# A two-layer hybrid block in fp32: another order of making the scaled blocks of the gated stage

## The chip, the cores and the metric

The kernel runs on 1 core of one Trainium2 chip. The metric is the device time of one execution in microseconds (us): before the change 2495.34 us, the median of 3 runs (2489.96 to 2497.64).

## The reference

One sequence of T = 1024 tokens with D = 1024 features goes through two layers. Layer 0 mixes tokens with two kinds of attention, layer 1 with a chunkwise mLSTM; both are followed by the same gated stage of hidden width 2816, whose beginning the change touches. Everything is fp32.

```python
for layer in range(DEPTH):                      # DEPTH = 2
    hn = rmsnorm(h, norm_mix[layer])
    h = h + mixer[layer](hn)                    # nsa_swa_mixer, then mlstm_mixer
    h = h + swiglu(rmsnorm(h, norm_ffn[layer]),
                   ffn_w_gate[layer], ffn_w_up[layer], ffn_w_down[layer])
return rmsnorm(h, final_norm)

def rmsnorm(x, g):
    return x * rsqrt(mean(x * x, axis=-1) + RMS_EPS) * g
def swiglu(x, wg, wu, wd):
    return (silu(x @ wg) * (x @ wu)) @ wd
```

## The kernel before

**Layout.** Activations lie transposed: 8 chunks of 128 features (on the partitions) by two token halves of 512, `h[hf][c]`. In the trace these tiles are named `r`.

**Products.** An fp32 product is made of three TensorE matmuls, high part by high part, high by low, low by high. The high part is a cast on ScalarE (`hi_copy`, L119), the low part a subtraction on VectorE that reads the cast (`lo_sub`, L124). So every operand and every weight costs one instruction on each of these engines before TensorE can use it. Operands split in this way are tiles `y`, weights split in this way `wh` (four chunks of weights, four such tiles in turn) and `whl` (eight chunks). Raw weights, `ws`, are loaded by SyncE's queue (L137).

**The gated stage** takes the hidden features 128 at a time, `m` = 0 to 21, in this program order:

- `ffn_head`: m = 0 and 1 on token half 0. The operand here was already split, without the factor 1/rms; the factor comes in behind the product (L284). Products go to `pg` and `pu` (L179 to L181).
- `rb(hf)` makes that factor for a half: a matmul with a matrix of ones sums the squares (`nrm`, L267), VectorE L269, ScalarE Ln (L271) and Exp (L272), each with a table load, then VectorE L274, L275, L277 into `consts`.
- `operands`, first part: for half 1, each chunk is multiplied in place by its norm weight and 1/rms (L953), all eight chunks, in the order 0, 4, 1, 5 and so on; then the eight results are split (L119, L124).
- `gated_rest`: m = 0 and 1 on half 1, 4 products of 24 matmuls, tiles `pr` (L983 to L985), each out of two halves of weights that are split when they are called for.
- `operands`, the rest: half 0 is scaled and one of its two blocks split, and the sums and differences of blocks (tiles `m`, L961 to L972) that the next step needs are made and split.
- `gated2`, m = 2 to 20 in steps of two: `wino` makes a 2 x 2 block product out of 7 instead of 8 block products (Winograd's form), for gate and for up. The seven operand blocks come in the order B11, T2, T1, B21, T3, T4, B22; B.. are blocks of the scaled input, T.. sums of them. A product is 12 matmuls into tiles `wb`, on lines L983 to L985 too. Their weights are sums of quarters of the raw weights (tiles `s`, L997) or the quarters, split one by one ahead of each product.

**What sets the order.** A scheduler turns the program order into one in-order queue for each engine, and adds the semaphore waits. An instruction that waits holds everything behind it on its engine. In layer 0 the second head (m = 1) stands in between the last products of the mixer; in layer 1 the mixer is done before `ffn_head` begins.

Of the kernel before, what the change touches and what calls it, by code (L numbers as in the profile page):

```python
# [25 lines left out]
NC = D // P  # L26
# [10 lines left out]
class Net:  # L37
# [753 lines left out]
    def mixer_ab(self):  # L791
# [3 lines left out]
        with tc.tile_pool(name="at", bufs=1) as self.at:  # L795
# [42 lines left out]
            next(last)  # L838
            head = self.ffn_head(0)
            next(head)  # L840
            for step in last:
                if step:
                    self.square(self.h[1][step[0]], 1)
            next(head)

    def ab_out(self, chunks, hfs):

# [94 lines left out]
        self.hi_copy(hi, x, "act")  # L942
        self.lo_sub(lo, x, hi)

    def operands(self, layer):

        nc = self.nc
        self.B = {}
        b = {}
        for hf in (1, 0):  # L950
            for c in (0, 4, 1, 5, 2, 6, 3, 7):
                x = b[c // 4, hf, c % 4] = self.h[hf][c]
                nc.vector.scalar_tensor_tensor(x, x, self.v("nf", layer * NC + c), self.rb(hf), op0=OP.mult, op1=OP.mult)  # L953
            for k in range(2):
                if hf or k == 0:
                    for j in range(4):
                        self.operand(f"B{k + 1}{hf + 1}", j, b[k, hf, j])
            yield
        t1, t2 = self.four(), self.four()
        for j in range(4):  # L960
            nc.vector.tensor_sub(t1[j], b[0, 1, j], b[0, 0, j])  # L961
            nc.vector.tensor_sub(t2[j], b[1, 1, j], t1[j])
            self.operand("T2", j, t2[j])
        for j in range(4):
            self.operand("T1", j, t1[j])
        for j in range(4):
            self.operand("B21", j, b[1, 0, j])
# [6 lines left out]
        yield  # L974
# [12 lines left out]
    def wino(self, st, out):  # L987
# [14 lines left out]
        def prod(ps, w, n, first=True):  # L1002
            self.half_products(ps, w, self.B[n], first)

        c11, u2, u3, c22 = self.four()
        a = bank()
        prod(a, a11, "B11")
        nc.scalar.copy(u3, a)
        s1, s2 = pair()
        combine(s1, a21, a22, OP.add)  # L1010
        combine(s2, s1, a11, OP.subtract)
        b = bank()
        prod(b, s2, "T2")
        nc.vector.tensor_add(u2, u3, b)
        c = bank()
        prod(c, s1, "T1")
        prod(a, a12, "B21", False)
        out(0, 0, a, c11)
        s3, s4 = pair()
        combine(s3, a11, a21, OP.subtract)  # L1020
# [11 lines left out]
        out(0, 1, u2, u2)  # L1032
        return (c11, u2), (u3, c22)

    def gated2(self, wg, wu, m):
# [12 lines left out]

        g = self.wino(sts[0], gate)
        self.wino(sts[1], up)  # L1050

    def gated_rest(self, wg, wu):
# [3 lines left out]
        for i in range(2):  # L1056
# [7 lines left out]
            nc.vector.tensor_mul(u, g, p[1])  # L1064
            self.hid_out(u, i, 1)

    def ffn(self, layer, last, head=False):
        nc, a = self.nc, self.a
        wg, wu, wd = (a[f"ffn_w_{n}"][layer] for n in ("gate", "up", "down"))
        if last:  # L1070
            self.park_tokens()
        else:
            for hf in range(2):
                for c in range(NC):
                    nc.sync.dma_start(self.spill[c][:, hf * H5:(hf + 1) * H5], self.h[hf][c])
# [12 lines left out]
        if last:  # L1088
# [490 lines left out]
```

## Time and profile before

| | before |
|---|---|
| median of 3 runs | 2495.34 us (2489.96 to 2497.64) |
| the profiled execution, its own time | 2500.09 us |
| its span in the trace | 2498.4 us |
| mean granted TensorE clock, share of full | 0.978 |
| busy: TensorE, VectorE, ScalarE, GpSimd | 95%, 65%, 36%, 20% of the span |

The profiled execution is one more run, 4.75 us above the median. Its own time is 1.7 us more than the span that its instructions cover. Engines are named as in the profile: PE is TensorE (PEld its weight loads), DVE VectorE, ACT ScalarE, POOL GpSimd, SP SyncE. A row of a timeline gives the start, the duration from first start to last end, and in brackets the idle time before it with what ended it. Matmul records last longer than the distance from one to the next, so pace is read from the distance of starts.

### The profile page before, as it was taken

How to read it: one execution, taken by the hardware profiler on the slowest of the kernel's cores; microseconds unless marked ns; L12 is line 12 of the kernel's file. 1: busy time of each engine (PE TensorE's matmuls, PEld its weight loads, DVE VectorE, ACT ScalarE, POOL GpSimd, SP SyncE). 2: the span in 40 equal slices, each digit the busy share in tenths (PEclk: the TensorE clock that was granted, in tenths of full speed). 3: DMA queues.
4: the chain of work that ended last, by engine and by line, in shares of the span. 5: the costliest groups of instructions: out<-in, count | busy, mean ns of one | idle time of the engine just before them, and what ended most of it. 6: DMA issues, size and time to landing. Idle time of an engine off the chain costs nothing.

```text
span 2498.4 us, 29577 instructions
## 1 busy us (share of the span) xinstructions
PE 2377.8 (95%) x10729; PEld 1899.5 (76%) x10729; DVE 1630.7 (65%) x2817; ACT 894.9 (36%) x1851; POOL 503.7 (20%) x606
## 2 busy tenths in 40 slices
PE   7999998998869999999999999999979999999998
PEld 5778776776658888887777788888857888887886
DVE  6545766687786666668876554554386666567867
ACT  5234655566252222222222344332253232222222
POOL 3134654444300000003322111111100000002322
PEclk9999989999989999999999999999989999999999
DMA  5623742211423433449333211122233434348443
GB/s 188 196 66 110 210 109 70 77 53 30 140 74 121 166 123 130 150 153 325 121 135 100 62 43 38 38 70 86 65 121 102 148 106 159 127 170 290 137 146 114
DMA packets 246757, 304.20 MB, mean 122 GB/s; under 512 B 19076, under 2 KB 157524, under 8 KB 246612
## 3 DMA queue, kind: packets, MB, share of 16 engines
q1 hardware_dynamic: 246612, 302.31, 37.5%
q8 instruction: 85, 1.39, 0.2%
q14 instruction: 60, 0.49, 0.1%
HBM read 218.33 MB, written 83.90 MB: 121 GB/s over the span
## 4 chain that ended last, share of the span: by engine, by line
PE 78%; DVE 8%; POOL 5%; issue 4%; ACT 3%; DMA 2%; SPq 0%; DVEq 0%; POOLq 0%; ACTq 0%
PE dn L1153 14%; PE wb L983 10%; PE wb L985 10%; PE wb L984 10%; PE acc L181 4%; PE acc L180 4%; PE acc L179 4%; PE acc L190 2%; PE acc L188 2%; PE acc L189 2%; PE T L701 2%; PE S L610 2%; POOL e L684 2%; PE po L695 1%; PE po L696 1%
## 5 line engine op out<-in xcount | busy, mean ns | idle before, releaser
L985 PE MATMUL wb<-y,wh 128*128 128x512 f32 x1120 | 442.3, 395 | 19.9 <-DVE wh L124 19.9
L983 PE MATMUL wb<-y,wh 128*128 128x512 f32 x1120 | 442.9, 395 | 1.3 <-DVE m L1023 1.2
L984 PE MATMUL wb<-y,wh 128*128 128x512 f32 x1120 | 443.0, 396 | 0.0
L117 POOL TENSOR_SCALAR wo<-ws 128x1024 fp32r<-128x1024 f32 x84 | 124.1, 1489 | 1114.1 <-DMA ws<-in_ffn_w_down 507.1
L985 PEld LDWEIGHTS wb<-y,wh 128*128 128x128 f32 x1120 | 211.7, 189 | 69.6 <-DVE wh L124 20.8
L983 PEld LDWEIGHTS wb<-y,wh 128*128 128x128 f32 x1120 | 211.4, 189 | 53.2 <-issue 4.3
L984 PEld LDWEIGHTS wb<-y,wh 128*128 128x128 f32 x1120 | 211.4, 189 | 48.1
L1153 PE MATMUL dn<-xo,wo 128*128 128x512 f32 x924 | 220.0, 401 | 6.2 <-DVE wo L124 6.1
L1153 PE MATMUL dn<-wo,xo 128*128 128x512 f32 x924 | 215.7, 395 | 2.2 <-ACT xo L119 2.1
L1153 PEld LDWEIGHTS dn<-xo,wo 128*128 128x128 f32 x924 | 176.9, 192 | 49.3 <-DVE wo L124 7.4
L1153 PEld LDWEIGHTS dn<-wo,xo 128*128 128x128 f32 x924 | 173.8, 188 | 44.0 <-issue 2.5
L179 PE MATMUL acc<-x,whl 128*128 128x512 f32 x416 | 170.4, 410 | 0.0
L180 PE MATMUL acc<-x,whl 128*128 128x512 f32 x416 | 166.3, 400 | 0.0
L181 PE MATMUL acc<-x,whl 128*128 128x512 f32 x416 | 165.4, 398 | 0.0
L188 PE MATMUL acc<-x,whl 128*128 128x512 f32 x384 | 158.2, 412 | 4.0 <-DMA x<-os 2.6
L189 PE MATMUL acc<-x,whl 128*128 128x512 f32 x384 | 155.3, 404 | 3.3 <-DMA x<-os 2.0
L684 POOL TENSOR_SCALAR e<-e,st 128x256 f32<-128x256 f32 (+7 forms) x192 | 121.6, 652 | 173.2 <-ACT oc L716 40.0
L124 DVE TENSOR_TENSOR wh<-ws,wh 128x512 fp32r<-128x512 f32 x136 | 93.0, 687 | 94.1 <-ACT wh L119 94.1
L190 PE MATMUL acc<-x,whl 128*128 128x512 f32 x384 | 153.6, 400 | 0.7 <-DVE whl L124 0.7
L119 ACT CAST xo<-hb 128x1024 fp32r<-128x1024 f32 x84 | 79.3, 975 | 205.5 <-PE dn L1153 134.9
L706 DVE TENSOR_TENSOR eh<-T,eh 128x512 fp32r<-128x512 f32 (+1 forms) x178 | 120.4, 687 | 48.5 <-ACT eh L705 47.1
L610 PE MATMUL S<-kv,qa 128*128 128x256 f32 (+3 forms) x528 | 124.4, 331 | 10.2 <-ACT ec L627 2.9
(335 smaller groups left out, 4414.8 us busy)
## 6 DMA issues: line engine op xcount, KB each, us to landing
ws<-in_ffn_w_down SPq DMA_DIRECT2D x34, 1024.0 KB
ws<-in_ffn_w_gate SPq DMA_DIRECT2D x22, 1024.0 KB
ws<-in_ffn_w_up SPq DMA_DIRECT2D x22, 1024.0 KB
sd<-m SPq DMA_DIRECT2D x22, 1024.0 KB
hs<-m SPq DMA_DIRECT2D x80, 256.0 KB
qa<-qs SPq DMA_DIRECT2D x128, 128.0 KB
hb<-hs SPq DMA_DIRECT2D x16, 1024.0 KB
ws<-sd SPq DMA_DIRECT2D x16, 1024.0 KB
```

Of the source, the lines that this page charges most:

```text
L179: nc.tensor.matmul(ps, w[:, 0, k], xh, start=(start and k == 0), stop=False)
L180: nc.tensor.matmul(ps, w[:, 0, k], xl, start=False, stop=False)
L181: nc.tensor.matmul(ps, w[:, 1, k], xh, start=False, stop=(stop and k == n - 1))
L188: self.nc.tensor.matmul(ps, w[:, 0, i], xh, start=i == 0, stop=False)
L189: self.nc.tensor.matmul(ps, w[:, 0, i], xl, start=False, stop=False)
L190: self.nc.tensor.matmul(ps, w[:, 1, i], xh, start=False, stop=i == len(xs) - 1)
L610: nc.tensor.matmul(p[:, at + c:at + c + k.shape[1]], qq[:, r * P:(r + 1) * P], k, start=i == 0, stop=i == 1, skip_group_check=True)
L684: self.last_scale = nc.gpsimd.tensor_scalar(es[r][:, :w], es[r][:, :w], f[:, r:r + 1], 0.0, op0=OP.mult, op1=OP.add)
L983: nc.tensor.matmul(ps, t[:, 0, k], xh, start=first and k == 0, stop=False, skip_group_check=True)
L984: nc.tensor.matmul(ps, t[:, 0, k], xl, start=False, stop=False, skip_group_check=True)
L985: nc.tensor.matmul(ps, t[:, 1, k], xh, start=False, stop=last and k == 3, skip_group_check=True)
L1153: nc.tensor.matmul(ps[i], l, r, start=first and k == 0 and q == 0, stop=end and k == 10 and q == 2, skip_group_check=True)
```

## The change

Three things are done in another order. (1) `rb(1)` is called right behind the first head, and the parking of `h` in memory behind it, ahead of the scaling. (2) `operands` becomes `scaled(layer, hf)`, which scales one chunk and splits it at once, chunks in the order 0 to 7, with half 1 ahead of the second head and half 0 behind it, both ahead of `gated_rest`; and `sums`, which makes the sums of blocks. (3) `sums` is called inside the first `gated2`, behind the splitting of the weights of its first four products (`half_parts` for a11, s2, s1, a12), no longer ahead of it. The number of instructions on each engine stays the same.

```diff
@@ mixer of layer 0
             head = self.ffn_head(0)
             next(head)
+            self.B = {}
             for step in last:
                 if step:
                     self.square(self.h[1][step[0]], 1)
+            self.rb(1)
+            for hf in range(2):
+                self.park(hf)
+            self.scaled(0, 1)
             next(head)
+            self.scaled(0, 0)
@@
-    def operands(self, layer):
-        nc = self.nc
-        self.B = {}
-        b = {}
-        for hf in (1, 0):
-            for c in (0, 4, 1, 5, 2, 6, 3, 7):
-                x = b[c // 4, hf, c % 4] = self.h[hf][c]
-                nc.vector.scalar_tensor_tensor(x, x, self.v("nf", layer * NC + c), self.rb(hf), op0=OP.mult, op1=OP.mult)
-            for k in range(2):
+    def scaled(self, layer, hf):
+        for k in range(2):
+            for j in range(4):
+                x = self.h[hf][4 * k + j]
+                self.nc.vector.scalar_tensor_tensor(x, x, self.v("nf", layer * NC + 4 * k + j), self.rb(hf),
+                                                    op0=OP.mult, op1=OP.mult)
                 if hf or k == 0:
-                    for j in range(4):
-                        self.operand(f"B{k + 1}{hf + 1}", j, b[k, hf, j])
-            yield
+                    self.operand(f"B{k + 1}{hf + 1}", j, x)
+
+    def sums(self):
+        nc = self.nc
+        b = {(k, n, j): self.h[n][4 * k + j] for k in range(2) for n in range(2) for j in range(4)}
         t1, t2 = self.four(), self.four()
...
-    def half_products(self, ps, w, x, first=True, last=True):
+    def half_parts(self, w):
         t = self.small_w()
         self.hi_copy(t[:, 0], w, "act")
         self.lo_sub(t[:, 1], w, t[:, 0])
+        return t
+
+    def half_products(self, ps, w, x, first=True, last=True, t=None):
+        if t is None:
+            t = self.half_parts(w)
@@ wino
+        t = [None] * 4
+        if between:
+            t[0] = self.half_parts(a11)
         s1, s2 = pair()
         combine(s1, a21, a22, OP.add)
         combine(s2, s1, a11, OP.subtract)
+        if between:
+            t[1:] = [self.half_parts(w) for w in (s2, s1, a12)]
+            between()
@@ ffn
         if not head:
-            for _ in self.ffn_head(layer):
-                pass
-        steps = self.operands(layer)
-        next(steps)
+            if last:
+                self.park_tokens()
+            else:
+                for hf in range(2):
+                    self.park(hf)
+            self.B = {}
+            steps = self.ffn_head(layer)
+            next(steps)
+            self.scaled(layer, 1)
+            next(steps)
+            self.scaled(layer, 0)
         self.gated_rest(wg[:, :2 * P], wu[:, :2 * P])
-        for _ in steps:
-            pass
         for m in range(2, 22, 2):
-            self.gated2(wg[:, m * P:(m + 2) * P], wu[:, m * P:(m + 2) * P], m)
+            self.gated2(wg[:, m * P:(m + 2) * P], wu[:, m * P:(m + 2) * P], m, self.sums if m == 2 else None)
```

What the queues hold, at three places. The first is VectorE in layer 0, from the second head to the scaled chunks of half 1. Before, `u` and `pu` belong to the head, `r` and `rm` to the chunks and to `rb`:

```order
L284 TENSOR_TENSOR u<-pu,consts 128x512
L922 TENSOR_TENSOR u<-g,u 128x512
L269 TENSOR_SCALAR rm<-nrm 128x512
L274 TENSOR_TENSOR rm<-rm,r_6919 128x512
L275 SCALAR_TENSOR_TENSOR rm<-rm,r_6919 128x512
L277 SCALAR_TENSOR_TENSOR consts<-rm,r_6919 128x512
L953 SCALAR_TENSOR_TENSOR r<-r,consts 128x512 x8
L124 TENSOR_TENSOR y<-r,y 128x512 x8
L124 TENSOR_TENSOR wh<-ws,wh 128x512
```

In the change the same engine at the same place, first the rows that make 1/rms:

```order
L269 TENSOR_SCALAR rm<-nrm 128x512
L124 TENSOR_TENSOR whl<-ws,whl 128x1024
L274 TENSOR_TENSOR rm<-rm,r_6835 128x512
L124 TENSOR_TENSOR wh<-ws,wh 128x512
L275 SCALAR_TENSOR_TENSOR rm<-rm,r_6835 128x512
L284 TENSOR_TENSOR g<-pg,consts 128x512
L277 SCALAR_TENSOR_TENSOR consts<-rm,r_6835 128x512
```

and then, behind one more `wh`, the rows of the chunks:

```order
L956 SCALAR_TENSOR_TENSOR r<-r,consts 128x512 x3
L124 TENSOR_TENSOR y<-r,y 128x512 x3
L956 SCALAR_TENSOR_TENSOR r<-r,consts 128x512 x3
L124 TENSOR_TENSOR y<-r,y 128x512 x3
L956 SCALAR_TENSOR_TENSOR r<-r,consts 128x512 x2
L284 TENSOR_TENSOR u<-pu,consts 128x512
L124 TENSOR_TENSOR y<-r,y 128x512 x2
L928 TENSOR_TENSOR u<-g,u 128x512
L124 TENSOR_TENSOR y<-r,y 128x512 x4
L124 TENSOR_TENSOR wh<-ws,wh 128x512 x4
```

L953 has become L956. The factor stands ahead of the head's two rows `u`, with one split of gated-rest weights `wh` inside it and one behind it; scaling and splitting take turns, and four chunks of half 0 (`y` x4) stand ahead of the next four `wh`.

The second place is VectorE in layer 1. Before, two pairs of `wh` (the weights of `gated_rest`) stand ahead of the factor of half 1:

```order
L953 SCALAR_TENSOR_TENSOR r<-r,consts 128x512 x3
L124 TENSOR_TENSOR wh<-ws,wh 128x512 x2
L953 SCALAR_TENSOR_TENSOR r<-r,consts 128x512 x3
L284 TENSOR_TENSOR u<-pu,consts 128x512
L269 TENSOR_SCALAR rm<-nrm 128x512
L922 TENSOR_TENSOR u<-g,u 128x512
L274 TENSOR_TENSOR rm<-rm,r_14685 128x512
L275 SCALAR_TENSOR_TENSOR rm<-rm,r_14685 128x512
L277 SCALAR_TENSOR_TENSOR consts<-rm,r_14685 128x512
L953 SCALAR_TENSOR_TENSOR r<-r,consts 128x512 x8
L124 TENSOR_TENSOR y<-r,y 128x512 x8
L124 TENSOR_TENSOR wh<-ws,wh 128x512
```

In the change, from the end of the factor on:

```order
L277 SCALAR_TENSOR_TENSOR consts<-rm,r_14618 128x512
L956 SCALAR_TENSOR_TENSOR r<-r,consts 128x512 x4
L124 TENSOR_TENSOR y<-r,y 128x512 x3
L956 SCALAR_TENSOR_TENSOR r<-r,consts 128x512 x3
L124 TENSOR_TENSOR y<-r,y 128x512 x3
L956 SCALAR_TENSOR_TENSOR r<-r,consts 128x512 x2
L284 TENSOR_TENSOR u<-pu,consts 128x512
L124 TENSOR_TENSOR y<-r,y 128x512 x2
L928 TENSOR_TENSOR u<-g,u 128x512
L124 TENSOR_TENSOR y<-r,y 128x512 x4
L956 SCALAR_TENSOR_TENSOR r<-r,consts 128x512 x2
L124 TENSOR_TENSOR wh<-ws,wh 128x512 x4
```

The first `wh` of `gated_rest` now stands behind all of these, and the factor and its `nrm` matmul ahead of the second head's products.

The third place is ScalarE in layer 0 around the first `gated2`. `m` are the sums of blocks and the results of products, `s` the sums of weights. Before, all casts of sums stand ahead of the first weights:

```order
L119 CAST y<-m 128x512 x4
L119 CAST y<-r 128x512 x4
L119 CAST y<-m 128x512 x8
L119 CAST wh<-s 128x512 x2
L119 CAST wh<-ws 128x512
L1008 COPY m<-wb 128x512
L119 CAST wh<-s 128x512
```

In the change, from the last of the first four weights (`wh<-ws`) to the weights of T3 (the first `wh<-s` here):

```order
L119 CAST wh<-ws 128x512
L119 CAST y<-r 128x512 x2
L1028 COPY m<-wb 128x512
L119 CAST y<-m 128x512 x6
L1058 ACTIVATE m<-wb 128x512
L119 CAST y<-m 128x512 x2
L119 CAST wh<-s 128x512
```

Four weights moved ahead of the sums; the weights of the fifth product, T3, stand behind the casts of T3 and T4 and behind the silu L1058 of the result that comes out of the fourth product.

## Rows read from the trace of the kernel before

**Rows 1.** The page: busy time of each engine, and the chain's shares.

```profile
PE 2377.8 (95%) x10729; PEld 1899.5 (76%) x10729; DVE 1630.7 (65%) x2817; ACT 894.9 (36%) x1851; POOL 503.7 (20%) x606
...
PE 78%; DVE 8%; POOL 5%; issue 4%; ACT 3%; DMA 2%; SPq 0%; DVEq 0%; POOLq 0%; ACTq 0%
```

**Rows 2.** Waits of 640 to 780 us, layer 0: us in total, times, longest.

```profile
PE wb L985 <- DVE wh L124: 10.0, 1, 10.0
```

**Rows 3.** Windows: PE, PEld, DVE, ACT, POOL busy; granted clock, DMA share, GB/s.

```profile
696.00:712.00 16.00, 4.45 (x10) 3.12 (x11) 13.22 (x21) 10.07 (x17) 0.00 (x0) 0.57 0.27 82
...
732.00:746.00 14.00, 4.05 (x11) 2.93 (x10) 13.90 (x25) 5.83 (x11) 0.00 (x0) 0.63 0.05 19
...
1831.00:1849.00 18.00, 6.90 (x17) 4.91 (x17) 15.86 (x26) 10.88 (x17) 0.00 (x0) 0.62 0.04 15
...
1868.00:1883.00 15.00, 5.05 (x13) 3.85 (x13) 15.00 (x26) 6.63 (x12) 0.00 (x0) 0.66 0.05 17
```

**Rows 4.** Timeline of PE in layer 0.

```profile
694.90 1.02 PE L267 MATMUL nrm<-consts 128*128 128x512 f32 x2
704.18 1.22 PE L983 MATMUL pr<-y,wh 128*128 128x512 f32 x2 [8.25 <-ACT y L119]
708.77 0.80 PE L984 MATMUL pr<-y,wh 128*128 128x512 f32 x1 [3.37 <-DVE y L124]
709.36 0.63 PE L985 MATMUL pr<-y,wh 128*128 128x512 f32 x1
709.79 0.63 PE L983 MATMUL pr<-y,wh 128*128 128x512 f32 x1
...
742.52 0.80 PE L985 MATMUL wb<-y,wh 128*128 128x512 f32 x1 [9.95 <-DVE wh L124]
...
755.05 0.39 PE L984 MATMUL wb<-y,wh 128*128 128x512 f32 x1
755.28 0.39 PE L985 MATMUL wb<-y,wh 128*128 128x512 f32 x1
```

**Rows 5.** Timeline of PE in layer 1.

```profile
1830.11 1.02 PE L267 MATMUL nrm<-consts 128*128 128x512 f32 x2
1838.85 1.22 PE L983 MATMUL pr<-y,wh 128*128 128x512 f32 x2 [7.72 <-ACT y L119]
1843.44 0.80 PE L984 MATMUL pr<-y,wh 128*128 128x512 f32 x1 [3.37 <-DVE y L124]
1844.03 0.63 PE L985 MATMUL pr<-y,wh 128*128 128x512 f32 x1
...
1878.15 0.79 PE L985 MATMUL wb<-y,wh 128*128 128x512 f32 x1 [9.95 <-DVE wh L124]
...
1891.38 0.40 PE L985 MATMUL wb<-y,wh 128*128 128x512 f32 x1
```

**Rows 6.** Timeline of DVE in layer 0.

```profile
684.00 0.69 DVE L257 TENSOR_TENSOR consts<-consts,sqt 128x512 f32<-128x512 f32 x1
...
702.72 5.39 DVE L953 SCALAR_TENSOR_TENSOR r<-r,consts 128x512 f32<-128x512 f32 x8
708.03 4.90 DVE L124 TENSOR_TENSOR y<-r,y 128x512 fp32r<-128x512 f32 x8
```

**Rows 7.** Timeline of ACT in layer 0.

```profile
691.14 1.15 ACT L119 CAST wh<-ws 128x512 fp32r<-128x512 f32 x2 [7.52 <-DMA ws<-in_ffn_w_gate]
...
698.59 1.28 ACT L272 ACT_TABLE_LOAD   x1
699.88 0.63 ACT L272 ACTIVATE r<-r 128x512 f32<-128x512 f32 x1
703.51 0.62 ACT L119 CAST y<-r 128x512 fp32r<-128x512 f32 x1 [3.00 <-DVE r L953]
```

**Rows 8.** Timelines of DVE and ACT in layer 1.

```profile
1822.98 1.14 ACT L119 CAST wh<-ws 128x512 fp32r<-128x512 f32 x2 [2.45 <-DMA ws<-in_ffn_w_gate]
...
1837.39 5.39 DVE L953 SCALAR_TENSOR_TENSOR r<-r,consts 128x512 f32<-128x512 f32 x8
```

More of the change, by code (lines that the diff above doesn't have):

```diff
@@ L943, in operand @@
         self.lo_sub(lo, x, hi)
-    def operands(self, layer):
-        nc = self.nc
-        self.B = {}
-        b = {}
-        for hf in (1, 0):
-            for c in (0, 4, 1, 5, 2, 6, 3, 7):
-                x = b[c // 4, hf, c % 4] = self.h[hf][c]
-                nc.vector.scalar_tensor_tensor(x, x, self.v("nf", layer * NC + c), self.rb(hf), op0=OP.mult, op1=OP.mult)
-            for k in range(2):
-                if hf or k == 0:
-                    for j in range(4):
-                        self.operand(f"B{k + 1}{hf + 1}", j, b[k, hf, j])
-            yield
+    def scaled(self, layer, hf):
[4 more added lines that the diff above has]
+                                                    op0=OP.mult, op1=OP.mult)
+                if hf or k == 0:
+                    self.operand(f"B{k + 1}{hf + 1}", j, x)
+    def sums(self):
+        nc = self.nc
+        b = {(k, n, j): self.h[n][4 * k + j] for k in range(2) for n in range(2) for j in range(4)}
         t1, t2 = self.four(), self.four()
@@ L973, in operands @@
             self.operand("T4", j, t2[j])
-        yield
-    def half_products(self, ps, w, x, first=True, last=True):
-        nc = self.nc
+    def half_parts(self, w):
         t = self.small_w()
@@ L985, in half_products, with wino @@
             nc.tensor.matmul(ps, t[:, 1, k], xh, start=False, stop=last and k == 3, skip_group_check=True)
-    def wino(self, st, out):
+    def wino(self, st, out, between=None):
         nc = self.nc
@@ L1000, in bank, with prod @@
             return self.ps.tile([P, H5], F32, name="wb", bufs=6)
[L1002 to L1008, printed above, removed]
+        def prod(ps, w, n, first=True, t=None):
+            self.half_products(ps, w, self.B[n], first, t=t)
+        t = [None] * 4
+        if between:
+            t[0] = self.half_parts(a11)
         s1, s2 = pair()
@@ L1011, in wino @@
         combine(s2, s1, a11, OP.subtract)
+        if between:
+            t[1:] = [self.half_parts(w) for w in (s2, s1, a12)]
+            between()
+        c11, u2, u3, c22 = self.four()
+        a = bank()
+        prod(a, a11, "B11", t=t[0])
+        nc.scalar.copy(u3, a)
         b = bank()
-        prod(b, s2, "T2")
+        prod(b, s2, "T2", t=t[1])
         nc.vector.tensor_add(u2, u3, b)
         c = bank()
-        prod(c, s1, "T1")
-        prod(a, a12, "B21", False)
+        prod(c, s1, "T1", t=t[2])
+        prod(a, a12, "B21", False, t[3])
         out(0, 0, a, c11)
@@ L1033, in wino, with gated2 @@
         return (c11, u2), (u3, c22)
-    def gated2(self, wg, wu, m):
+    def gated2(self, wg, wu, m, between=None):
         nc = self.nc
@@ L1047, in up @@
                 self.first_up = t
-        g = self.wino(sts[0], gate)
+        g = self.wino(sts[0], gate, between)
         self.wino(sts[1], up)
@@ L1065, in gated_rest, with park @@
             self.hid_out(u, i, 1)
+    def park(self, hf):
+        for c in range(NC):
+            self.nc.sync.dma_start(self.spill[c][:, hf * H5:(hf + 1) * H5], self.h[hf][c])
     def ffn(self, layer, last, head=False):
@@ L1069, in ffn @@
         wg, wu, wd = (a[f"ffn_w_{n}"][layer] for n in ("gate", "up", "down"))
[L1070 to L1075, printed above, removed]
-        if not head:
-            for _ in self.ffn_head(layer):
-                pass
-        steps = self.operands(layer)
-        next(steps)
+        if not head:
+            if last:
[9 more added lines that the diff above has]
+            self.scaled(layer, 0)
         self.gated_rest(wg[:, :2 * P], wu[:, :2 * P])
-        for _ in steps:
-            pass
         for m in range(2, 22, 2):
-            self.gated2(wg[:, m * P:(m + 2) * P], wu[:, m * P:(m + 2) * P], m)
+            self.gated2(wg[:, m * P:(m + 2) * P], wu[:, m * P:(m + 2) * P], m, self.sums if m == 2 else None)
             for k in (m // 2 - 1, 10)[:1 + (m == 18)]:
```

## The prediction, made before the changed kernel was run

> **What bounds the kernel now.** I read the page first, for the engine that sets the pace: PE is busy for 95% of the span and carries 78% of the chain that ended last [rows 1]. So time can be won only where PE stands still or runs at its lower clock. The change touches two such places in each layer, which I then looked for in the waits, and read off in PE's timeline.
>
> At the first place, PE has finished the second head and the `nrm` matmul, and waits for the first split chunk of half 1: 8.25 us in layer 0, then 3.37 us more for that chunk's low part [rows 4]. In layer 1 these are 7.72 and 3.37 [rows 5]. What is late is visible on the other engines: the factor's chain through ACT, with a table load of 1.28 us ahead of Exp [rows 7], and then eight scalings on DVE before the first subtraction may start [rows 6]. At the second place PE has done two matmuls of the first `gated2` and waits 9.95 us for the low part of its first weights [rows 2, 4, 5], since these stand in DVE's queue behind all the sums. Idle in sum: 21.6 us in layer 0 and 21.0 us in layer 1.
>
> After each stall the clock is low as well. The windows around the four places show granted shares of 0.57, 0.63, 0.62 and 0.66, a mixture of the two levels, 1.2 and 2.4 GHz [rows 3]. Behind the first stall in layer 0 matmuls start every 0.43 us; later every 0.23 us [rows 4]. I counted 7, 8, 11 and 10 matmuls at the slow pace behind the four stalls, each 0.2 us dearer: about 3 us for layer 0 and 4 for layer 1. All that the change can reach is thus 42.6 + 7 = 50 us.
>
> **What the change costs and saves.** No instruction is added, so the price is a walk through the queues in their new order, with durations from the rows. A scaling costs (708.03 - 702.72)/8 = 0.664 us, a subtraction (4.90 - 0.69)/7 = 0.60 us [rows 6], a matmul 0.23 us. The matmul `nrm` only changes its place; the head ends when it did.
>
> *Layer 0, first place.* The last square is added by 684.7 [rows 6]. With `nrm` right behind it, L269, Ln, a table load of 1.28 and Exp bring L274 to 690.0. Next in DVE's queue stands the low part of a `gated_rest` weight, which waits for a cast, which waits for the load that landed at 691.14 [rows 7]: cast 0.63 and subtraction 0.6 end at about 692.5. This holds L275 and all behind it for some 2 us. Four more instructions (L275, the head's `g`, L277, a second `wh`) at 0.6 end at 694.9, where the first scaling starts, 7.8 us before its 702.72 [rows 6]. From that start to PE's first matmul it took 704.18 - 702.72 = 1.46 us [rows 4, 6], so PE starts at 696.3, and the wait of 8.25 shrinks to under half a microsecond.
>
> But now DVE sets the pace. From 694.9 it has eight scalings, eight subtractions and the head's two rows `u` (5.3 + 4.8 + 1.2 = 11.3, to 706.2), then four subtractions of half 0 and the next `wh` (3.0), to 709.3. Until then PE gets through the 28 matmuls whose weights are ready, and stands for about 3 us at the end. The remaining 68 of the 96 take 15.7 us, and some seven at the lower clock 1.4 more: `gated_rest` ends at 726.5.
>
> *Layer 0, second place.* B11, T2, T1 and B21 have their weights early, since these stand ahead of the sums: four products of 12 matmuls, 11.1 us, to 737.6. T3's weights are the next thing late. DVE's queue up to their subtraction holds 52 instructions at 0.60 from about 710.4, which gives 741.7; and ACT's cast for them stands behind a silu of B21's result, two casts of T4's sums, and their turns with DVE, which gives 743.5. I take 743.5, since the cast is needed first, and keep 741.7 for the range. So PE stands about 6 us at T3. T3's third matmul was at 755.28 [rows 4]: 11.8 earlier, less eight matmuls at the lower clock (1.6), gives **10.2 us** for layer 0 (13.6 by DVE's count; 8 if the 2 us at the weight load double).
>
> *Layer 1, first place.* With `nrm` between the heads, the first chunk can be scaled at about 1829.3, where it was 1837.39 [rows 8]: the two tables ahead of Exp, one more cast (load landed at 1822.98 [rows 8]) and five scalings of half 0 lie in between, all beside the second head. The wait of 7.72 goes. But four `wh` that stood ahead of the factor now stand behind the chunks. DVE has ten scalings, twelve subtractions and two rows `u` first: 6.6 + 7.2 + 1.2 = 15.1, to 1844.3; the first `wh` ends at 1845.0. PE can do four matmuls (those needing only high weights) before that, and goes on at about 1845.05. Before, its third was at 1844.03 [rows 5]. So at this place nothing is won, and one microsecond is lost; the stall has only changed its releaser, from the chunk to the weight. The 92 left take 21.2 us, and twelve at the lower clock 2.4 more: 1868.7.
>
> *Layer 1, second place.* Four products of 11.1 us in all end at 1879.8. By DVE's queue, which has no wait to sit out here, T3's weights are ready at about 1879.6: just in time. T3's third matmul comes at 1880.3, and was at 1891.38 [rows 5]: **11.05 us**. If the weights miss by as much as in layer 0's second estimate (1.8 us) and matmuls at the lower clock follow (1.6), 7.6 are left; if `wh` come earlier than counted, up to 4 us of the first stall go too, which makes 15.
>
> *Unpriced edits.* Parking ahead of the scaling keeps its order on SP's queue. The four weights held at once use all four `wh` tiles; the fourth, a12, can be cast only when `gated_rest`'s last product lets go its tile at 726.5, and DVE's queue reaches it at about the same time (it also waits there for that product, L1081); this is in the 743.5.
>
> The sum is 10.2 + 11.05 = 21.2 us. Against the profiled execution's own 2500.09 us this gives 2478.9. That execution lay 4.75 us above the median of the runs, so I predict **2474 us**, with 2466 to 2480 as this case's own range (the bounds 8 + 7.6 and 13.6 + 15).
>
> **A rule against a row.** Ahead of Exp stand table loads, in layer 1 two. The row shows a load of 1.28 us and Exp 0.01 us behind its end [rows 7], so I count 1.28 each. The Trainium skill, in "ScalarE: Activation LUTs", "What ACT_TABLE_LOAD costs", adds a drain of about 1.38 us to a load of 1.283, 2.66 for a switch. By this the factor in layer 1 would come 2.8 us later and the sum be an estimated 18.5; the row shows no such drain behind the load, and I leave it out.
>
> **Rivals.**
>
> *A. The stalls only move* (0.10). For it: in layer 1 the first stall stays as it is by my own walk, and in layer 0 DVE had 13.22 of 16 us busy around the stall [rows 3], so it has little room. If T3 and T4 wait some 7 us more in each layer than I count, 21 shrinks to 7 or less: 2488 to 2495. Against: the sums were ahead of the first product and 9.95 us behind; now four products (11.1 us of PE) cover them.
>
> *B. The clock stays at its lower level* (0.04). In layer 0 PE will work in short pieces, paced by DVE, from 696 to 709, and stand again at T3. If it stays at 0.43 us per matmul up to T3, about 115 matmuls cost 0.2 more, 23 us, and the gain is gone: 2494 to 2497. Against: after each of the four stalls it took 7 to 11 matmuls to return to 0.23. The Trainium skill, in "TensorE: Matmul & The Clock Gate", "A second HAM failure mode: psum-queue depth-cycling", describes an engine that idles briefly between groups of matmuls often enough to swing between the two levels; by this rule B would be the case, but the trace agrees only in so far as a stall is followed by matmuls at the slower pace.
>
> *C. Slower: the weight load now holds the factor* (0.05). The cast of `gated_rest`'s first weight stands ahead of Exp (layer 1) or its subtraction ahead of L275 (layer 0), which before did not wait for a load. Each microsecond that this load lands later moves scaling, splits and sums by one. The gain is gone when it lands about 10.6 us later in each layer, and the kernel slower by 0.3% (7.5 us, about what a measurement of it can tell from no change) at 14: 2503 and more. For it: ACT already stood 7.52 us for this load in layer 0 [rows 7]. Against: SP's order is the same, and what lets the load start is not later.
>
> *D. More than counted* (0.15). If DVE slips `wh` and T3's weights through without my turn-taking, T3's wait in layer 0 (6 us and what the clock loses behind it) and 3 to 4 us at layer 1's first place go: 30 to 36 in all, 2459 to 2465.
>
> **How the numbers follow.** My own case has 0.66. It and D lie more than 0.3% (2487.9) below the median, and of A the best part (0.02): faster 0.83. The rest of A and B: same 0.12. C: slower 0.05. The range from 2459 to 2489 takes in D, my case and the nearer part of A; B, C and the rest of A, 0.17, stay outside.
>
> **What would show it.** Right: PE's 8.25 and 7.72 for `y` gone; in layer 0 a few short waits for `y` and one of about 3 for `wh`; in layer 1 a stall of 10 us or more at the third to fifth matmul of `gated_rest`, released by DVE `wh`; no wait at the first matmuls of `wb`, but about 6 at T3 in layer 0 and nearly none in layer 1. Wrong: L275 held for long behind the weights' load, granted shares under 0.6 up to T3, or waits at T4 and B22 that add up to as much as the old 9.95.

## The result, and the profile after

The changed kernel takes 2471.37 us (median of 4 runs, 2467.70 to 2475.77), beside 2494.35 us before (4 runs): 23.0 us less, a ratio of 0.991 with a 95% interval of 0.9896 to 0.9924. A second measurement, e9 below, gave 2470.01 beside 2494.26. Forecast were 2474 us and faster.

The page of the profiled execution (2475.77 us, span 2474.0) has the same busy times as before, only on a shorter span [rows 1]:

```profile
PE 2374.9 (96%) x10729; PEld 1895.6 (77%) x10729; DVE 1630.4 (66%) x2817; ACT 896.7 (36%) x1851; POOL 501.9 (20%) x606
```

TensorE's waits of more than 2 us at the changed places, from the windows of 640 to 780 us (layer 0: the first two) and of 1770 to 1890 us (layer 1: the third), each with its total in us, how many times, and the longest. The 9.95 us for `wb` and the 8.25 and 7.72 for `y` [rows 2, 4, 5] are gone; three others stand in their place:

```profile
PE wb L993 <- ACT wh L119: 4.8, 1, 4.8
...
PE pr L995 <- DVE wh L124: 2.8, 1, 2.8
...
PE pr L995 <- DVE wh L124: 12.3, 1, 12.3
```

PE's timeline in layer 0 of the changed kernel, the rows that answer to [rows 4]. L983 to L985 have become L993 to L995:

```profile
680.36 1.02 PE L267 MATMUL nrm<-consts 128*128 128x512 f32 x2
...
690.93 0.40 PE L181 MATMUL pu<-x,whl 128*128 128x512 f32 x1
692.38 0.51 PE L993 MATMUL pr<-y,wh 128*128 128x512 f32 x1 [1.06 <-ACT y L119]
693.66 0.59 PE L994 MATMUL pr<-y,wh 128*128 128x512 f32 x1 [0.77 <-DVE y L124]
...
705.43 0.79 PE L995 MATMUL pr<-y,wh 128*128 128x512 f32 x1 [2.83 <-DVE wh L124]
706.03 0.63 PE L993 MATMUL pr<-y,wh 128*128 128x512 f32 x1
...
723.83 0.40 PE L993 MATMUL wb<-y,wh 128*128 128x512 f32 x1
...
739.87 0.79 PE L993 MATMUL wb<-y,wh 128*128 128x512 f32 x1 [4.77 <-ACT wh L119]
...
750.88 0.39 PE L993 MATMUL wb<-y,wh 128*128 128x512 f32 x1
```

`nrm` lies inside the second head. The first product of `gated_rest` follows the head after 1.06 us, a stall of 2.83 us for a weight comes after 28 matmuls, the first `gated2` starts at 723.83 with no wait, and the next wait is at T3. The row at 739.87 is T3's first matmul, 750.88 the first behind all seven products. In layer 1, the rows that answer to [rows 5]:

```profile
1819.11 0.39 PE L181 MATMUL pu<-x,whl 128*128 128x512 f32 x1
...
1833.25 0.80 PE L995 MATMUL pr<-y,wh 128*128 128x512 f32 x1 [12.33 <-DVE wh L124]
...
1867.71 0.39 PE L993 MATMUL wb<-y,wh 128*128 128x512 f32 x1
...
1876.06 0.39 PE L993 MATMUL wb<-y,wh 128*128 128x512 f32 x1
```

No wait at the head's end and none at T3 (1867.71), but 12.33 us ahead of the fifth matmul of `gated_rest`.

**A yardstick that leaves the rest of the program out.** The kernel's other parts move by some us from one execution to the next: the first matmul of layer 0's head, ahead of every edit, started at 654.03 us in the trace of before, at 650.05 in that of after, and between 646.14 and 653.19 in the experiments. The trace of before is the latest of all, and there is only this one of it, of an execution 5.7 us above the median of its runs. So I compare stretches: from the end of the head's last matmul to the first matmul behind the seven products of the first `wino`. The trace of before has the latter at

```profile
763.15 0.39 PE L983 MATMUL wb<-y,wh 128*128 128x512 f32 x1
...
1899.25 0.39 PE L983 MATMUL wb<-y,wh 128*128 128x512 f32 x1
```

and the head's end (`nrm`) at 694.90 + 1.02 and 1830.11 + 1.02 [rows 4, 5]: 67.2 us in layer 0 and 68.1 in layer 1. After, the stretches are 750.88 - 691.33 = 59.6 and 1876.06 - 1819.50 = 56.6. So **7.7 us** came from layer 0 and **11.6 us** from layer 1.

| run | median us | against before, 95% interval | stretch won, layer 0 | layer 1 |
|---|---|---|---|---|
| changed kernel | 2471.37 | 0.9896 to 0.9924 | 7.7 | 11.6 |
| e9, changed kernel again | 2470.01 | 0.9888 to 0.9918 | 9.6 | 10.9 |
| e1, weights ahead of sums alone | 2485.96 | 0.9933 to 0.9965 | 3.6 | 4.2 |
| e2, blocks early alone | 2486.75 | 0.9941 to 0.9970 | 2.9 | 3.8 |
| e3, layer 0 alone | 2486.68 | 0.9947 to 0.9975 | 7.8 | -1.6 |
| e4, scale all, then split | 2470.49 | 0.9881 to 0.9908 | 10.9 | 10.8 |
| e5, T3's weights early | 2470.24 | 0.9885 to 0.9915 | 11.6 | 11.8 |
| e6, rest weights first | 2474.93 | 0.9904 to 0.9932 | 10.1 | 10.8 |
| e7, low parts on GpSimd | 2475.46 | 0.9913 to 0.9938 | 9.8 | 7.2 |
| e8, e4 + e5 + e7 | 2468.68 | 0.9884 to 0.9913 | 11.3 | 10.2 |
| e10, e4 + e5 | 2466.14 | 0.9878 to 0.9908 | 13.8 | 11.8 |
| e11, e4 + e5 + e6 | 2466.24 | 0.9864 to 0.9901 | 15.1 | 13.9 |

The median of before beside e1 to e4 was 2496.39 us, beside e5 to e8 2494.81, beside e9 to e11 2494.26. The stretches are of one profiled execution each, the medians of 4 or 5 runs. In layer 0 the changed kernel, e3, e6 and e9 run the same code, and their stretches won differ by up to 2.4 us: smaller differences between two rows show nothing by themselves.

### The profile page after: what moved, and what is told of

It reads as the page before. It is cut to its first block, busy times and chain, and to the rows that moved or that the text cites. A ratio compares the mean times of both kernels' runs of the same rounds, so it can differ in the third digit from the quotient of the medians.

```text
span 2474.0 us, 29578 instructions
## 1 busy us (share of the span) xinstructions
PE 2374.9 (96%) x10729; PEld 1895.6 (77%) x10729; DVE 1630.4 (66%) x2817; ACT 896.7 (36%) x1851; POOL 501.9 (20%) x606
## 4 chain that ended last, share of the span: by engine, by line
PE 67%; DVE 6%; issue 4%; POOL 4%; ACT 2%; DMA 1%; SPq 0%; DVEq 0%; POOLq 0%; ACTq 0%
PE dn L1173 14%; PE wb L993 10%; PE wb L994 10%; PE wb L995 10%; PE acc L181 4%; PE acc L180 4%; PE acc L179 4%; POOL e L684 1%; PE T L701 1%; PE S L610 1%; DVE y L124 1%; POOL x L245 1%; PE po L695 1%; PE po L696 1%; PE pr L995 1%
## 5 line engine op out<-in xcount | busy, mean ns | idle before, releaser
L993 PE MATMUL wb<-y,wh 128*128 128x512 f32 x1120 | 442.6, 395 | 6.1 <-ACT wh L119 4.8
L995 PE MATMUL wb<-y,wh 128*128 128x512 f32 x1120 | 441.0, 394 | 0.0
L993 PEld LDWEIGHTS wb<-y,wh 128*128 128x128 f32 x1120 | 210.8, 188 | 58.8 <-ACT wh L119 5.2
L995 PEld LDWEIGHTS wb<-y,wh 128*128 128x128 f32 x1120 | 211.1, 188 | 49.7 <-DVE wh L124 0.7
```

## The experiments

The theory that the experiments test: VectorE is the bound from the scaled blocks up to T3's weights, so a stall is worth not its own length but what VectorE's queue gains. The rival: each stall is worth its own length.

**e1: the weights ahead of the sums, alone.** In `ffn` and in the mixer, 1/rms and the blocks are made as before (the added argument `True` asks for the old order of scaling). Here, as in the cuts below, `...` marks lines left out:

```diff
...
-            steps = self.ffn_head(layer)
-            next(steps)
-            self.scaled(layer, 1)
-            next(steps)
-            self.scaled(layer, 0)
+            for _ in self.ffn_head(layer):
+                pass
...
+        self.scaled(layer, 1, True)
         self.gated_rest(wg[:, :2 * P], wu[:, :2 * P])
+        self.scaled(layer, 0, True)
```

> Only part 3 of the change: the weights of the first four products ahead of the sums; the scaled blocks and 1/rms as before. Theory 1 (VectorE bounds the stretch from the scaled blocks up to the weights of T3): the first stalls stay as before (about 8.2 and 3.4 us in layer 0, 7.7 and 3.4 in layer 1), the 9.95 us stall ahead of the first product goes, but T3's weights are then late, by 4 to 6 us in each layer, with matmuls at the lower clock behind it. So 4 to 6 us are won in each layer, 8 to 12 in all. Rival (each stall is worth its own length): both stalls of 9.95 us and their matmuls at the lower clock go, 20 to 23 us in all, and T3 does not wait.

Measured: 10.4 us less than before. PE's rows at T3 in the two layers:

```profile
743.56 0.80 PE L998 MATMUL wb<-y,wh 128*128 128x512 f32 x1 [4.75 <-ACT wh L119]
...
1875.71 0.79 PE L998 MATMUL wb<-y,wh 128*128 128x512 f32 x1 [4.74 <-ACT wh L119]
```

The 9.95 us are gone, and half of them stands again at T3. These are the theory's 8 to 12 us, not the rival's 20 to 23.

**e2: the blocks early, alone.** The sums are made ahead of all weights of the first `gated2` again:

```diff
+        self.sums()
         for m in range(2, 22, 2):
-            self.gated2(..., m, self.sums if m == 2 else None)
+            self.gated2(..., m)
```

> Only parts 1 and 2: 1/rms beside the head and scaled blocks ahead of gated_rest; the sums again ahead of all weights of the first gated2. Theory 1: in layer 0 VectorE starts 7.8 us earlier and all behind it with it, less a wait or two, 3 to 6 us; in layer 1 gated_rest does not start earlier (a stall of 12 us at its fifth matmul for the low part of a weight), but the sums behind it are done a few us earlier, 2 to 4 us; a stall of 9 to 13 us for wh stays ahead of the first wb product's third matmul in both layers. 5 to 10 us won in all. Rival (each stall is worth its own length): the 8.25 and 7.72 us go in full, 16 us.

Measured: 9.6 us less than before, stretches 2.9 and 3.8. The stall ahead of the first product's third matmul is back, and layer 1 has two:

```profile
733.66 0.79 PE L995 MATMUL wb<-y,wh 128*128 128x512 f32 x1 [11.76 <-DVE wh L124]
...
1836.69 0.79 PE L995 MATMUL pr<-y,wh 128*128 128x512 f32 x1 [12.33 <-DVE wh L124]
...
1865.66 0.80 PE L995 MATMUL wb<-y,wh 128*128 128x512 f32 x1 [5.25 <-DVE wh L124]
```

TensorE's waits in the stretch add up to 17.2 us in layer 0 and 17.8 in layer 1, where they were 21.6 and 21.0 before: most of what went at the head's end stands further back. The theory had 9 to 13 us ahead of the first product's third matmul in both layers; in layer 1 it is 5.25. e1 and e2 win 14.5 us of the stretches together, the whole change 19.2 and 20.5: each part alone leaves a longer wait behind it. The medians (10.4 + 9.6 = 20.0 us, beside 23.0 and 24.2) don't separate with their intervals; that the two are worth more together rests on these traces.

**e3: layer 0 alone.** Layer 1 has the old order, with the sums ahead of the weights:

```diff
-            steps = self.ffn_head(layer)
...
+            for _ in self.ffn_head(layer):
+                pass
+            self.scaled(layer, 1, True)
         self.gated_rest(wg[:, :2 * P], wu[:, :2 * P])
+        if not head:
+            self.scaled(layer, 0, True)
+            self.sums()
...
-            self.gated2(..., m, self.sums if m == 2 else None)
+            self.gated2(..., m, self.sums if m == 2 and head else None)
```

> The whole change in layer 0, layer 1 as before. This tells apart where the gain arose. Theory 1: the matmuls of layer 0 from the end of the head to behind T3 give 7.5 to 10 us, layer 1 the same waits as before (7.7, 3.4, 9.95), in all 7.5 to 10 us; the part of the changed kernel's gain that stood in its trace ahead of the change (4.6 us up to the last square of layer 0) is scatter from one execution to the next. Rival: that 4.6 us belongs to the change (something in the mixer is scheduled better), then 12 to 14 us.

Measured: 9.7 us less; layer 0's stretch won 7.8, as in the changed kernel; layer 1's waits are the old ones (7.65 and 3.37 us for `y`), the one for `wb` a little longer:

```profile
1866.10 0.79 PE L1005 MATMUL wb<-y,wh 128*128 128x512 f32 x1 [11.75 <-DVE wh L124]
```

The time that the changed kernel's trace had won ahead of the edits looks like scatter: its 4.0 us at the first head's first matmul are 3.0 here, and 0.8 to 7.9 in the others, in no relation to what was edited; and the 9.7 us are the theory's 7.5 to 10, not the rival's 12 to 14.

**e4: scale all, then split.** This stands in place of scaling and splitting by turns, in both layers:

```diff
+        if whole:
+            for c in (0, 4, 1, 5, 2, 6, 3, 7):
+                x = self.h[hf][c]
+                self.nc.vector.scalar_tensor_tensor(x, x, self.v("nf", layer * NC + c), self.rb(hf),
+                                                    op0=OP.mult, op1=OP.mult)
+            for k in range(2):
+                if hf or k == 0:
+                    for j in range(4):
+                        self.operand(f"B{k + 1}{hf + 1}", j, self.h[hf][4 * k + j])
+            return
```

> As the changed kernel, but all eight chunks of a half are scaled before the first is split, in the order of before. Theory 1: what counts is when VectorE is through with the chunks and the weights behind them, not the order in between; the work is the same, so the same time as the changed kernel within 3 us, with a longer first wait for y (4 us) and a shorter one for wh. Rival (scaling and splitting by turns is what feeds the matmuls): 4 us slower in each layer than the changed kernel, 8 in all.

Measured: 2470.49 us, as the changed kernel. The waits lie elsewhere:

```profile
698.36 0.80 PE L1004 MATMUL pr<-y,wh 128*128 128x512 f32 x1 [3.57 <-DVE y L124]
...
1827.66 0.80 PE L1005 MATMUL pr<-y,wh 128*128 128x512 f32 x1 [8.53 <-DVE wh L124]
```

In layer 0 one stall of 3.57 us after two matmuls, for the first chunk's low part, takes the place of the 2.83 after 28. The turns win nothing; layer 0's stretch is even 1 to 3 us shorter without them, which the medians don't resolve.

**e5: T3's weights ahead of T4's sums.** `sums` stops ahead of T4, and `wino` goes on:

```diff
...
         combine(s3, a11, a21, OP.subtract)
-        prod(b, s3, "T3", False)
+        t3 = self.half_parts(s3) if between else None
+        if between:
+            next(between)
+        prod(b, s3, "T3", False, t3)
```

> As the changed kernel, but the weights of T3 are summed and split ahead of the sums of T4 in both layers. Theory 1 (VectorE is the bound up to T3; the place of T3's weights in its queue decides): in layer 0 the wait of 4.77 us ahead of T3 shrinks to 0 to 1 us and the matmuls at the lower clock behind it go (2 us), less a new wait of 2 to 3 us for T4's blocks; layer 1, where T3 did not wait, is unchanged. 2 to 5 us less than the changed kernel. Rival (the wait ahead of T3 is one for ScalarE's cast, behind the silu of B21's result): the cast still comes late, no gain.

Measured: layer 0 wins 11.6 us (the changed kernel 7.7 and 9.6), layer 1 as before the edit. PE's first wait in layer 0's `gated2` is now at T4's third matmul:

```profile
743.47 0.50 PE L997 MATMUL wb<-y,wh 128*128 128x512 f32 x1 [2.09 <-DVE wh L124]
```

The median, 2470.24, doesn't differ from the changed kernel's; the trace shows the 4.77 us gone and 2.09 come. The rival (ScalarE's cast comes late whatever VectorE does) is out: here the cast for T3 began at 730.35 us and its product at 737.99.

**e6: the weights of `gated_rest` first, in layer 1.** `rest_weights` loads them and splits the first four:

```diff
             self.scaled(layer, 1)
             next(steps)
+            ready = self.rest_weights(wg, wu)
             self.scaled(layer, 0)
-        self.gated_rest(wg[:, :2 * P], wu[:, :2 * P])
+        self.gated_rest(wg[:, :2 * P], wu[:, :2 * P], ready)
```

> As the changed kernel, but in layer 1 the first four weights of gated_rest are called for ahead of half 0's blocks, so that their low parts stand earlier in VectorE's queue. Theory 1 (VectorE's whole count up to T3 decides): the stall of 12.33 us at the fifth matmul of gated_rest goes, gated_rest ends some 10 us earlier, and T3 waits for its weights about as much longer, since VectorE comes to them at the same time: within 2 us of the changed kernel. Rival (each stall is worth its own length): 10 to 14 us less.

Measured: nothing won (10.8 us in layer 1, 2474.93 us). There is no wait ahead of the fifth matmul any more, the longest in `gated_rest` is 1.06 us ahead of the 53rd, and T3, which had no wait in layer 1, has one:

```profile
1830.85 0.51 PE L995 MATMUL pr<-y,wh 128*128 128x512 f32 x1 [1.06 <-DVE wh L124]
...
1860.69 0.80 PE L993 MATMUL wb<-y,wh 128*128 128x512 f32 x1 [8.24 <-ACT wh L119]
```

This is the clearest of the runs: `gated_rest` starts its last matmul 26.9 us behind the head's end instead of 36.8 and 37.5 (the changed kernel's two traces), and none of these ten microseconds reaches the end of the stretch.

**e7: the low parts of `gated_rest`'s weights on GpSimd.** Only `gated_rest` asks for `pool`:

```diff
...
-        self.lo_sub(t[:, 1], w, t[:, 0])
+        if pool:
+            self.nc.gpsimd.tensor_tensor(t[:, 1], w, t[:, 0].bitcast(F32), op=OP.subtract)
+        else:
+            self.lo_sub(t[:, 1], w, t[:, 0])
```

> As the changed kernel, but the eight low parts of gated_rest's weights are subtracted by GpSimd, which has nothing else to do there, in both layers. VectorE loses 8 x 0.60 = 4.8 us of work in each. Theory 1 (VectorE's count is the bound): the stalls of 2.83 (layer 0) and 12.33 us (layer 1) for wh go, T3 comes about 4.8 us earlier by VectorE's count, and in layer 0 VectorE's own waits for TensorE (2.5 us) go too: 4 to 7 us in each layer, 8 to 14 less than the changed kernel. Rival (the engines share what they read and write through, or GpSimd's subtraction takes longer than a product: 128x256 took it 0.65 us, so 1.3 or more): VectorE's instructions become longer than 0.60, or TensorE waits for GpSimd, and nothing is won or up to 10 us lost.

Measured: 2475.46 us, layer 1's stretch about 4 us longer than the changed kernel's (4.4 and 3.7), layer 0's within the scatter. Here the rival was right. GpSimd's row and VectorE's beside it, in layer 0:

```profile
692.13 3.23 POOL L985 TENSOR_TENSOR wh<-ws,wh 128x512 fp32r<-128x512 f32 x2 [5.15 <-ACT wh L119]
...
710.56 4.78 POOL L985 TENSOR_TENSOR wh<-ws,wh 128x512 fp32r<-128x512 f32 x3 [5.86 <-ACT wh L119]
```

```profile
691.74 4.17 DVE L956 SCALAR_TENSOR_TENSOR r<-r,consts 128x512 f32<-128x512 f32 x3
695.83 1.88 DVE L124 TENSOR_TENSOR y<-r,y 128x512 fp32r<-128x512 f32 x3
...
710.67 3.50 DVE L967 TENSOR_TENSOR m<-r 128x512 f32<-128x512 f32 x2
714.09 0.68 DVE L1085 TENSOR_TENSOR u<-g,pr 128x512 f32<-128x512 f32 x1
```

Three scalings take 4.17 us beside GpSimd, 2.07 in the changed kernel; two sums 3.50 instead of 1.29. A subtraction takes GpSimd 1.65 us on average and relieves VectorE of 0.60. In layer 0 these stretched rows alone cost 2.10 + 2.21 us, and the next three scalings (4.12) 2.05 more: at least 6.4 us lost for 8 x 0.60 = 4.8 saved.

**e8: e4, e5 and e7 together**, with the three edits as they stand above.

> The changed kernel with all chunks of a half scaled before the first is split, T3's weights ahead of T4's sums, and the low parts of gated_rest's weights on GpSimd. Theory 1: the gains add as far as VectorE's count is the bound: about 3 us (layer 0) from the first, 2 to 5 from the second, 8 to 14 from the third: 12 to 20 us less than the changed kernel, 35 to 43 less than before. Rival (after one of them another engine is the bound): no better than the best of the three alone.

Measured: 26.1 us less than before, 11.3 and 10.2 us of the stretches; not the 35 to 43 of the theory, which had counted on e7. The rival's "no better than the best of the three alone" holds within what the runs resolve.

**e9 to e11: the changed kernel again, e4 with e5, and e4 with e5 and e6**, on one chip.

> The changed kernel itself, unaltered, beside the next two on the same chip. All theories: 20 to 25 us less than before; in layer 0 the number of matmuls at the lower clock behind the stalls is what scatters from one execution to the next (7 to 12 behind each).

> The changed kernel with all chunks of a half scaled before the first is split, and T3's weights ahead of T4's sums; GpSimd takes nothing. Theory 1 (VectorE's count is the bound): layer 0 gains some 3 us from the first and 2 to 4 from the second, layer 1 nothing: 3 to 7 us less than the changed kernel, and as good as or better than with GpSimd's help. Rival (what helped was GpSimd's share of the work): worse than with it, 2470 or more.

> As the one before, and in layer 1 the first four weights of gated_rest ahead of half 0's blocks. Theory 1: with T3's weights 5.4 us earlier in VectorE's queue the stall that the earlier gated_rest had moved to T3 (8.24 us) shrinks to 3 to 5 us, so layer 1 gains 2 to 5 us, 5 to 11 less than the changed kernel in all. Rival (VectorE's whole count up to T4 and its blocks decides): the wait only moves from T3 to T4, and layer 1 gains nothing.

Measured: 2470.01, 2466.14 and 2466.24 us; the last ran between 2457.09 and 2472.05. e10 without GpSimd's help is no worse than e8 with it. In layer 0 e10 keeps two short waits, in layer 1 e11 has two in place of the 8.24 us of e6:

```profile
697.03 0.79 PE L1006 MATMUL pr<-y,wh 128*128 128x512 f32 x1 [3.56 <-DVE y L124]
...
737.87 0.51 PE L1007 MATMUL wb<-y,wh 128*128 128x512 f32 x1 [2.09 <-DVE wh L124]
```

```profile
1845.27 0.57 PE L1005 MATMUL wb<-y,wh 128*128 128x512 f32 x1 [2.93 <-ACT wh L119]
...
1852.73 0.50 PE L1007 MATMUL wb<-y,wh 128*128 128x512 f32 x1 [2.11 <-DVE wh L124]
```

In these traces the order of e6 is worth 2 us in layer 1 once T3's weights stand ahead of T4's sums (2 to 5 were expected), and nothing before that; the medians, 0.1 us apart, don't show it. Both are about 28 us faster than before (1.1 to 1.2%) and about 4 us faster than the changed kernel beside them (3 to 7 and 5 to 11 were expected), a difference that the intervals (0.9878 to 0.9908 and 0.9864 to 0.9901 against 0.9888 to 0.9918) don't separate. The stretches won, 25.6 and 29.0 us against 20.5, point the same way, in one execution each, and e11's was the fastest of its five, 9 us below their median.

## Why the prediction was right, point by point

**The factor beside the head.** Right in both layers: `nrm` lies in the second head, the waits of 8.25 and 7.72 us are gone. In layer 0 VectorE was held by the weight's load as foretold, for 2.47 us (foretold: some 2); this is the first of these rows of the changed kernel; the other rows of VectorE and the last one, ScalarE's, are read further down:

```profile
687.92 0.69 DVE L124 TENSOR_TENSOR wh<-ws,wh 128x512 fp32r<-128x512 f32 x1 [2.47 <-ACT wh L119]
...
704.70 2.49 DVE L124 TENSOR_TENSOR wh<-ws,wh 128x512 fp32r<-128x512 f32 x4
...
710.11 0.69 DVE L968 TENSOR_TENSOR m<-r,m 128x512 f32<-128x512 f32 x1 [1.72 <-PE pr L995]
...
724.03 0.69 DVE L1081 TENSOR_TENSOR u<-g,pr 128x512 f32<-128x512 f32 x1
...
740.29 0.68 DVE L124 TENSOR_TENSOR wh<-s,wh 128x512 fp32r<-128x512 f32 x1
...
739.20 0.62 ACT L119 CAST wh<-s 128x512 fp32r<-128x512 f32 x1 [1.78 <-DVE s L1008]
```

**The new stalls in `gated_rest`.** 28 matmuls and then about 3 us for `wh` in layer 0: 28 and 2.83. Foretold for layer 1 were four matmuls, a stall, and nothing won: it is four matmuls, and then 12.33 us. Counted from the head's end, TensorE goes on at 1833.25 - 1819.50 = 13.8 us; the walk had 1845.05 - 1831.1 = 13.9. (The walk compared this with the start of the third matmul, and took 1844.03 for it; in [rows 5] that is the fourth, the third started at 1843.44. Its sum doesn't use that row.)

**T3 in layer 1.** "Just in time": the low part ends at 1866.77 + 0.68 = 1867.45, T3 starts at 1867.71 without a wait. The gain, 11.05 by the walk, is 11.6 and 10.9 in the two traces of the changed kernel, with 9 and 12 matmuls at the lower clock where the walk had twelve. VectorE had hardly a pause on the way; the windows of the changed kernel (columns as in [rows 3]) show it busy for 15.00 of 15, 18.80 of 19 and 17.00 of 17 us:

```profile
1819.00:1834.00 15.00, 2.46 (x9) 1.40 (x8) 15.00 (x25) 6.22 (x11) 0.00 (x0) 0.66 0.05 17
1834.00:1853.00 19.00, 19.00 (x77) 15.32 (x76) 18.80 (x32) 11.37 (x21) 0.00 (x0) 0.91 0.39 124
1853.00:1870.00 17.00, 17.00 (x74) 13.74 (x74) 17.00 (x30) 9.21 (x16) 0.00 (x0) 1.00 0.08 22
```

That is what e6 met: with VectorE full, a stall taken away up front comes back behind.

**T3 in layer 0.** Here the size was off. Foretold were 10.2 us with a wait of about 6; measured were 7.7 (the changed kernel), 7.8 (e3), 9.6 (e9) and 10.1 (e6), four traces of the same code in layer 0, with a wait of 4.77. Two terms of the sum were mis-sized:

- The matmuls at the lower clock. The walk had seven in `gated_rest` and eight behind T3. The changed kernel's trace has 12 behind the stall of 2.83 us and 11 behind T3, so the rest of `gated_rest` took 723.83 - 705.43 = 18.4 us (the walk: 17.2), and the 36 matmuls from T3 on 750.88 - 739.87 = 11.0 (the walk: the 8.3 of before and 1.6). e9's has 7 and 10, e6's 7 and 8, and they came out at 9.6 and 10.1. Seven more, behind the wait of 0.77 us at 693.66, cost nothing, since VectorE sets the pace there: from its first scaling to the end of the stall it is 14.5 us with them (690.93 to 705.43) and without them (692.12 to 706.62 in e9).
- The anchor of T3's weights. The walk counted VectorE's queue through from 710.4 us. But VectorE pauses for TensorE on the way (1.72 us at L968), and at L1081, which takes the last product of `gated_rest`, it waits for TensorE again, if only for 0.1 us (the product's last matmul starts at 723.60, L1081 at 724.03). From there to the subtraction for T3 it has 27 instructions, 740.29 - 724.03 = 16.3 us, and TensorE only 48 matmuls, 11.1 us. The sum of quarters that T3's cast needs stands three of them earlier; the cast waits 1.78 us for it (the ACT row above) and is done at 739.8, so ScalarE only hands VectorE's lateness on. The wait at T3 thus hangs on the end of `gated_rest`, not on how early VectorE began: it was 4.74 to 4.77 us in layer 0 of the changed kernel, e1, e3, e4, e6 and e9, and in layer 1 of e1, wherever these 27 stood. e5 took most of T4's sums and splits out of them, and the wait was gone. From the end of `gated_rest` to T3 it took 16.0 us, 1.0 less than the walk's 743.5 - 726.5.

Two smaller terms: the stall of 2.83 us ended 14.1 us behind the head's end (the walk: 13.4), and the walk set the start of T3's first matmul, 743.5, against the old start of its third, 755.28, where the first started at 754.82. Together 10.2 - 1.2 - 1.1 + 1.0 - 0.7 - 0.5 = 7.7, the measured gain. (T3's shorter wait, the +1.0, made up for a part of the rest without being foreseen.)

**The sum.** 21.2 us were foretold; the stretches give 19.2 and 20.5, the medians 23.0 and 24.2. The medians stand 1 to 5 us better against before than the stretches say, save for e6 and e11 (1 us worse); where these come from isn't shown, and the other parts of the program scatter by as much. That 2471.37 lies so near the forecast of 2474 is thus partly luck: layer 0 gave 2.5 us less than foretold, and 3.7 us of the median's 23.0 came from where the walk had nothing.

**The rivals.** A (the stalls only move) is what each half does by itself (e1, e2) and what e6 does, not the whole change. B (the lower clock up to T3) didn't come: in the changed kernel TensorE was back at 0.23 us per matmul after 7, 12, 11 and 9 of them. C (the load holds the factor) held VectorE for the 2.47 us in layer 0 (1.78 in e9), far from the 10.6 that would have taken the gain. D (30 to 36 us) is not in this kernel; e10 and e11 come near it with other orders, by 25.6 and 29.0 us of the stretches and 28 us of the medians, and don't reach it.

**The table loads.** Exp follows its load at once here too, and the load follows what stands ahead of it, as ScalarE's rows in layer 1 show:

```profile
1810.75 0.60 ACT L119 CAST wh<-ws 128x512 fp32r<-128x512 f32 x1
1811.37 1.28 ACT L272 ACT_TABLE_LOAD   x1
1812.67 0.64 ACT L272 ACTIVATE r<-r 128x512 f32<-128x512 f32 x1
```

No drain stands on either side of the load, and 1.28 us each was the right price.

## What to carry to other kernels

Before a stall is priced at its own length, sum up what the engine it waits for still has to do up to the next point where the two meet. If that engine is full, as VectorE is here in layer 1 from the scaled blocks to T3, a wait taken away at the front stands again behind, and only moving work past the meeting point (T4's sums behind T3's weights) or shortening it can show at the end. And where that engine itself waits for the first on the way, as in layer 0, count its queue from that point on. Two reorderings that look like two gains can be worth more together than apart (19.2 and 20.5 us beside 14.5 by the stretches here), since each alone leaves the other's wait longer.

## What the runs showed of the hardware

VectorE and GpSimd get in each other's way, and not with every instruction. VectorE's scalings and sums, which read two tiles in on-chip memory (SBUF), took 1.78 us each in e7's rows instead of 0.66 and 0.60 where they met GpSimd's subtractions (two of each three scalings; the third took 0.75 at most). Not stretched were L277, a row with two such tiles that met only the first 0.6 us of a subtraction (0.68 us at 1817.45), and L1085, which reads one of its two from a TensorE result (`pr`) and took 0.68 us at 714.09 with GpSimd at work until 715.34. The changed kernel's trace bears this out: VectorE's `eh<-T,eh`, with T a TensorE result, took 688 ns on average both with GpSimd at work for at least 80% of its time (71 times) and with GpSimd idle (75 times), while `wo<-ws,wo`, two SBUF tiles, took 1643 in the first case (14 times) and 1216 in the second (33 times). The Trainium skill, in "GPSIMD Engine Reference", "1. Specifications", says that GpSimd's way to on-chip memory is shared with VectorE and that VectorE's instructions with two inputs from there contend for it; the traces agree, and give the price: 6.4 us or more of VectorE's time in layer 0 for eight subtractions taken off it.

How many matmuls run at the lower clock behind a stall has little to do with the stall's length. They were 9, 12, 8 and 6 behind the same 12.33 us in layer 1 (changed kernel, e9, e2 and e5), and 7, none and none behind the same 0.77 or 0.78 us in layer 0 (changed kernel, e3 and e6). The windows behind the 0.77 and the 2.83 us of the changed kernel and behind the 0.78 of e3 show granted clocks of 0.54, 0.50 and 1.00, the lower of the two levels (1.2 GHz) in the first two, with a little of the upper in the first, and the upper one (2.4 GHz) in the third:

```profile
693.66:697.20 3.54, 3.54 (x9) 2.78 (x10) 3.54 (x6) 2.36 (x5) 0.00 (x0) 0.54 0.00 0
...
705.43:710.70 5.27, 5.27 (x12) 4.13 (x13) 3.55 (x6) 0.00 (x0) 0.00 (x0) 0.50 0.46 156
...
694.36:698.00 3.64, 3.01 (x11) 1.99 (x11) 3.64 (x6) 2.46 (x5) 0.00 (x0) 1.00 0.00 0
```

At 0.2 us each this is up to 2.6 us per stall (13 in e3 and e4), and most of the scatter between executions of the same code: the four traces of layer 0's code have 30, 25, 17 and 15 of them (changed kernel, e3, e9, e6) in stretches of 59.6, 59.4, 57.7 and 57.1 us.
